# A decoder layer in fp32: one weight split moved behind a bank's copy, and four squares spread out

## The chip, the cores and the metric

The kernel runs on one core of one Trainium2 chip. It is one launch that computes a whole decoder layer. The metric is the device time of that launch in microseconds. The core's engines run side by side, each through its own list of instructions in order: TensorE (PE) multiplies, ScalarE (ACT) and VectorE (DVE) work elementwise, GpSimd (POOL) and SyncE (SP) mostly issue DMAs. An instruction that waits holds up all that stand behind it on its engine.

## The reference

```python
def rms_norm(x, w):
    x32 = x.astype(jnp.float32)
    y = x32 * lax.rsqrt(jnp.mean(x32 * x32, axis=-1, keepdims=True) + EPS)
    return y.astype(x.dtype) * w

def swiglu(h, w_in, w_out):
    gate, up = jnp.split(h @ w_in, 2, axis=-1)
    return (jax.nn.silu(gate) * up) @ w_out
...
        x = x + 0.5 * swiglu(rms_norm(x, norm_ffn1_w[l]), ffn1_w_in[l], ffn1_w_out[l])
        x = x + hybrid_mixer(rms_norm(x, norm_mix_w[l]), ...)
        x = x + memory_cross_attention(rms_norm(x, norm_cross_w[l]), rms_norm(mem, norm_mem_w[l]), ...)
        x = x + 0.5 * swiglu(rms_norm(x, norm_ffn2_w[l]), ffn2_w_in[l], ffn2_w_out[l])
    return rms_norm(x, norm_final_w)
```

x is 512 tokens of 1024 float32 values, the hidden size of both feed-forward networks (FFN1 and FFN2) is 2816, there is one layer, and the memory has 256 tokens. The change touches the two feed-forward networks: their products with `w_in`, and the norm at the start of FFN2.

## The kernel before

**Precision by splitting.** Every float32 operand is split into an upper part in the reduced format fp32r and the lower rest: ScalarE copies the upper part (`wh`, `s31h`, `gh` and so on; the rows of line 155), VectorE subtracts it from the source (`wl`, `s31l`, `gl`; line 156). A product is then three matmuls: upper by upper, upper by lower, lower by upper. A weight tile is 128x1024, and the pools give three buffers each to `wh` and `wl` and six to the raw weights `wr`. So the split of a weight waits until the product three splits earlier has ended.

**A group of seven products.** The FFNs multiply by a scheme of Strassen's kind: `quad` makes a 2x2 block product from seven products instead of eight. Each is 24 matmuls. They run in the order "11" (into bank qa), S1 (qe), S2 (qb), "12" (qa), S3 (qb), S4 (qe), "22" (qb), and each has its own weight split. Between them stand copies of banks: qa is copied to qb after "11" (so that S2 adds to it), qe is saved as `p` after S1, and after S2 qb is saved as `u2` and subtracted from qe (line 300). Only after `u2` is read may S3 write qb. The sums of weights that the products need (`t2`, `t4`) come from VectorE, or, in FFN1, partly from a DMA that accumulates. There are 8 such groups in FFN1 and 11 in FFN2. After a group, `ffn_quads` multiplies by the norm's row, takes the SiLU and multiplies gate and up (lines 447 to 450, tiles `gate` and `th`); `block_tiles` then makes the split sums `g11`, `s31`, `s24` and `g` for the output product.

**The output product.** `out_blocks` does the same seven products for `w_out`, for a third of the hidden size at a time, in parts of two tiles. In FFN1's thirds the weight sums are made on the way: SP loads a part (line 1279), POOL issues an accumulating DMA onto it (line 1318 and, for the last sum, 1336), and VectorE adds the second operand of S2's sum (line 1328), which sets that operand's raw buffer free for a later load.

**The order of the work.** The program is emitted by generators that an `Order` interleaves by an estimated time. A list scheduler then sets the orders of PE, ScalarE and VectorE by its own estimates; SP and POOL keep the order of emission. `behind([...])` forces an instruction behind others of the same engine only. So a weight split under `behind([copy.ins])` has its ScalarE half tied behind that copy, and its VectorE half is free.

**The start of FFN2.** The last part of the cross attention's output (`turn(1)`) writes tiles 4 to 7 of x. The norm of FFN2 needs the squares of all eight tiles (`squared`, line 551), then a row of reciprocal roots (`row_from`, through two small matmuls into `nrow` and the copy of line 407), which the gate multiplies of the first group need. The first group of FFN2 is `fresh`: its first two products are emitted so that their last parts alternate.

Of the kernel before, what the change touches and what calls it, by code (L numbers as in the profile page):

```python
# [13 lines left out]
AF = mybir.ActivationFunctionType  # L14
# [6 lines left out]
KT = D // P  # L21
# [79 lines left out]
def body(tc, a, dbg=None):  # L101
# [13 lines left out]
    def nm(s):  # L115
        uid[0] += 1
        return f"{s}_{uid[0]}"

    def s2(s, dt=F32, shape=(P, T)):
        if math.prod(shape[1:]) <= T // 2:  # L120
            return sp.tile(list(shape), dt, tag="s1", name=nm(s), bufs=NHALF)
        return sp.tile(list(shape), dt, tag="s2", name=nm(s))
# [4 lines left out]
    def small(s, n, bufs=None):  # L127
        return tiny.tile([P, n], F32, tag=s, name=nm(s), bufs=bufs)

    def acc(s, shape=(P, T)):  # L130
        return acc_p.tile(list(shape), F32, tag="acc", name=nm(s))
# [8 lines left out]
    last, start, last_sum, recent, newest, newest_mm = [], [], [], [], [], []  # L140
    V, S, G = nc.vector, nc.scalar, nc.gpsimd
    od = Order()
# [5 lines left out]
    def transpose(out, x):  # L148
        od.t += 2 * (P + 8) / 2400
        nc.tensor.transpose(out, x, ident)  # L150

    def split_into(hi, lo, src, scale=None):
        if scale is None:
            return (
                S.activation(hi, src, AF.Copy),  # L155
                V.tensor_tensor(lo, src, hi.bitcast(F32), ALU.subtract),  # L156
            )
        return (
            S.activation(hi, src, AF.Copy, scale=scale),
            V.scalar_tensor_tensor(lo, src, scale, hi.bitcast(F32), ALU.mult, ALU.subtract),  # L160
        )
# [21 lines left out]
    @contextmanager  # L183
    def behind(ins):
        with ExitStack() as after:
            for i in ins:
                after.enter_context(tc.issue_after(i))
            yield

    H = T // 2  # L190
    S1, S2, S3, S4 = "S1", "S2", "S3", "S4"
# [37 lines left out]
    def add_product(ps, w, xs, which, first, ks=None):  # L229

        wh, wl = w
        n = len(xs)
        for f in range(2):
            out = ps[:, f * H : (f + 1) * H]
            for kp in ks or range(n):
                wc = slice((f * n + kp) * P, (f * n + kp + 1) * P)
                xh, xl = xs[kp][which]
                for j, (a_, b_) in enumerate(((wh, xh), (wh, xl), (wl, xh))):
                    od.t += (H + 32) / 2400
                    newest_mm[:] = [nc.tensor.matmul(out, a_[:, wc], b_, start=first and f == 0 and kp == 0 and j == 0, stop=kp == n - 1 and j == 2, skip_group_check=True).ins]  # L240
                yield

    def raw_w(src, *more):

        raw = wp.tile([P, D], F32, tag="wr", name=nm("wr"), bufs=6)
        nc.sync.dma_start(raw, src)
        for m in more:
            last_sum[:] = [G.dma_start(raw, m, accum_op=ALU.add).ins]
        return raw

    def split_w(raw):
        hi = wp.tile([P, D], R32, tag="wh", name=nm("wh"))
        lo = wp.tile([P, D], R32, tag="wl", name=nm("wl"))
        newest[:] = [split_into(hi, lo, raw)[0].ins]
        return hi, lo

    def quad(xs, src, ready, fresh=False):

        b12, b11, b22, b21 = src[0], src[1], src[2], src[3]
        m1 = raw_w(b11)
        if ready:
            t, t2, m2, m7, m3 = raw_w(ready[0]), raw_w(ready[1]), raw_w(b21), raw_w(b12, b22), raw_w(b22)
            t4 = m2
        else:
            t, m3, m2, m7 = raw_w(b12, b11), raw_w(b22), raw_w(b21), raw_w(b12, b22)  # L270
            t2 = t4 = t
        a_ps = acc("qa")
        e_ps = acc("qe")
        b_ps = acc("qb")
        w1, w5 = split_w(m1), split_w(t)
        second = list(newest)
        if fresh:

            n = len(xs)
            yield from add_product(a_ps, w1, xs, "11", True, range(n - 1))  # L280
            yield from add_product(e_ps, w5, xs, S1, True, range(n - 1))
            yield from add_product(a_ps, w1, xs, "11", False, range(n - 1, n))
            with behind(second):
                S.activation(b_ps, a_ps, AF.Copy)  # L284
            yield from add_product(e_ps, w5, xs, S1, False, range(n - 1, n))
        else:
            yield from add_product(a_ps, w1, xs, "11", True)
            with behind(second):
                S.activation(b_ps, a_ps, AF.Copy)
            yield from add_product(e_ps, w5, xs, S1, True)  # L290
        p5 = s2("p5")
        S.activation(p5, e_ps, AF.Copy)
        if not ready:
            V.tensor_tensor(t2, t, m3, ALU.add)
        yield from add_product(b_ps, split_w(t2), xs, S2, False)
        if not ready:
            V.tensor_tensor(t4, t2, m2, ALU.add)
        u2 = s2("u2")
        S.activation(u2, b_ps, AF.Copy)  # L299
        V.tensor_tensor(e_ps, e_ps, u2, ALU.subtract)  # L300
        yield from add_product(a_ps, split_w(m2), xs, "12", False)
        w7 = split_w(m7)
        if ready:
            V.tensor_tensor(t4, t2, m2, ALU.add)
        yield from add_product(b_ps, w7, xs, S3, False)
        c22 = s2("c22")
        V.tensor_tensor(c22, p5, b_ps, ALU.subtract)
        yield from add_product(e_ps, split_w(m3), xs, S4, False)
        yield from add_product(b_ps, split_w(t4), xs, "22", False)
        yield (a_ps, b_ps), (e_ps, c22)  # L310

# [15 lines left out]
    x, xf, wa = [], [], []  # L327
# [107 lines left out]
    def ffn_quads(xs, wq, st, nq, made, places, sums=None, fresh=False, prime=None):  # L435

        for q in range(nq):
            for out in quad(xs, next(wq), next(sums) if sums else None, fresh and q == 0):
                if out is None:
                    yield  # L440
            gs, us = out
            if prime and q == nq - 1:
                next(prime)
            gate, th = s4("gate"), s4("th")
            for i in range(2):
                row = st.row[:, None, i * H : (i + 1) * H].to_broadcast([P, 2, H])
                V.tensor_tensor(gate[:, 2 * i : 2 * i + 2], halves(gs[i]), row, ALU.mult)
            S.activation(gate, gate, AF.Silu)
            for i in range(2):
                V.tensor_tensor(th[:, places[i]], halves(us[i]), gate[:, 2 * i : 2 * i + 2], ALU.mult)  # L450
            made(th)
            yield
# [97 lines left out]
    def squared(k, src):  # L550
        S.activation(s2("junk"), src, AF.Square, accum_out=squares[:, k : k + 1])

    def row_from(st, apart, rows=1.2):
        both = small("nboth", 4, bufs=2)
        V.tensor_tensor(both, squares[:, :4], squares[:, 4:], ALU.add)
        yield from st.from_sums(both, apart, rows)
# [657 lines left out]
    st_2, xs_2, half = Stat(), [], {}  # L1214
# [20 lines left out]
    def turn(n, banks=None, summed=False):  # L1235

        pt = [bank("pxf") for bank in banks or [aux] * 4]
        for j in range(4):
            for tb in range(4):
                transpose(pt[tb][:, j * P : (j + 1) * P], x[4 * n + j][:, tb * P : (tb + 1) * P])  # L1240
        for tb in range(4):
            S.activation(x[4 * n + tb], pt[tb], AF.Copy)
            if summed:
                squared(4 * n + tb, x[4 * n + tb])
            yield
# [209 lines left out]
            yield from out_blocks(a[f"f2b{c}"], wsum[c], g, col4, ncol4, *((norm, store) if at_end else (None, None)), clean=c == 0)  # L1455

    def turn_last():
        yield from turn(1, summed=True)
        od.spawn(row_from(st_2, 8.0), 3.0)

    od.add(turn_last())
    od.add(ffn2())
    od.run()
# [88 lines left out]
```

## Time and profile before

| | |
|---|---|
| times of the runs | 1314.59, 1314.65, 1318.22 us (median 1314.65) |
| profiled execution | 1314.59 us, of which its span is 1312.7 us |
| TensorE busy | 1288.3 us, 98% of the span |
| VectorE, ScalarE busy | 968.9 us (74%), 708.2 us (54%) |
| granted TensorE clock, mean | 0.997 |
| DMA | 237.38 MB, mean 181 GB/s |

A busy share is an average over the span. Where one engine is busy 98%, what a change can bring is read from the few places where that engine waits, and from which instruction ended each wait. In rows of the profile, `qb<-s31h,wh` means that tile qb is written from tiles s31h and wh; numbers of buffers are left out. `[1.58 <-ACT u L299]` behind a row says that the engine was idle for 1.58 us before it, and that ScalarE's instruction of line 299 that wrote `u` ended this.

### The profile page before, as it was taken

The numbers are of one execution on the slowest core, as the hardware profiler recorded it, in microseconds if no ns is written. First come the engines' busy times: TensorE is split into PE (matmuls) and PEld (weight loads), VectorE is DVE, ScalarE is ACT, GpSimd is POOL, SyncE is SP. The second block draws the span as 40 slices with busy tenths as digits, with TensorE's granted clock in tenths as the row PEclk, the third lists the DMA queues.
The fourth block names the chain that finished last, engine by engine and source line by source line (L and its number), as shares of the span: only waits on it lengthen the run. The fifth ranks groups of instructions, "written<-read, shape, count | busy, mean of one in ns | idle before, by whom it ended". The sixth has DMA issues, their size and how long they took to land.

```text
span 1312.7 us, 20086 instructions
## 1 busy us (share of the span) xinstructions
PE 1288.3 (98%) x7708; PEld 1123.4 (86%) x7708; DVE 968.9 (74%) x1538; ACT 708.2 (54%) x1208; POOL 127.8 (10%) x157
## 2 busy tenths in 40 slices
PE   9999999999999999999999999999999999999996
PEld 7889988998887778777788877888889999989995
DVE  6987887787776676467867686645668878877886
ACT  7544564565754564346645465434375646555564
POOL 0001010001010011201003022020001000000001
PEclk9999999999999999999999999999999999999998
DMA  9366778876984434753466558683239776666762
GB/s 339 88 168 185 212 184 211 222 199 162 324 291 145 137 64 133 261 166 105 95 189 173 167 141 238 196 222 120 69 99 274 209 231 181 185 193 180 201 192 82
DMA packets 70415, 237.38 MB, mean 181 GB/s; under 512 B 8288, under 2 KB 9792, under 8 KB 69968
## 3 DMA queue, kind: packets, MB, share of 16 engines
q1 hardware_dynamic: 54352, 183.20, 41.7%
q0 software_dynamic: 13168, 45.67, 19.7%
q10 hardware_dynamic: 2800, 7.23, 1.7%
q8 instruction: 60, 0.98, 0.3%
q14 instruction: 35, 0.29, 0.1%
HBM read 233.92 MB, written 50.91 MB: 217 GB/s over the span
## 4 chain that ended last, share of the span: by engine, by line
PE 58%; issue 10%; DVE 4%; ACT 2%; DMA 2%; POOL 1%; POOLq 0%; ACTq 0%; DVEq 0%
PE pm L146 10%; PE qb L240 8%; PE qe L240 5%; PE qa L240 5%; PE pxbc L146 4%; PE ob L1298 3%; PE pcq L146 3%; PE pz L146 3%; PE oe L1298 2%; PE oa L1298 2%; PE pcv L146 2%; PE pq L146 2%; PE pv L146 1%; PE pk L146 1%; DMA wr<-in_f1b 1%
## 5 line engine op out<-in xcount | busy, mean ns | idle before, releaser
L155 ACT ACTIVATE wh<-wr 128x1024 fp32r<-128x1024 f32 (+1 forms) x329 | 334.2, 1019 | 359.3 <-issue 70.6
L156 DVE TENSOR_TENSOR wl<-wr,wh 128x1024 fp32r<-128x1024 f32 (+1 forms) x329 | 384.8, 1173 | 145.3 <-ACT wh L155 140.2
L777 ACT ACTIVATE ec<-ec,mn 128x512 f32<-128x512 f32 (+3 forms) x64 | 35.4, 554 | 33.7 <-DVE mn L776 33.7
L146 PE MATMUL pxbc<-hnh,wh 128*128 128x512 f32 x128 | 52.6, 411 | 0.0
L146 PE MATMUL pxbc<-hnh,wl 128*128 128x512 f32 x128 | 50.3, 393 | 0.0
L146 PE MATMUL pxbc<-hnl,wh 128*128 128x512 f32 x128 | 50.2, 392 | 0.0
L240 PE MATMUL qb<-s31h,wh 128*128 128x256 f32 x152 | 43.2, 284 | 3.2 <-ACT u L299 3.2
L240 PE MATMUL qb<-s24h,wh 128*128 128x256 f32 x152 | 43.1, 284 | 1.3 <-ACT qb L284 1.3
L240 PE MATMUL qb<-s24h,wl 128*128 128x256 f32 x152 | 43.1, 284 | 0.5 <-DVE wl L156 0.5
L240 PE MATMUL qe<-s31h,wl 128*128 128x256 f32 x152 | 43.1, 284 | 0.2 <-DVE wl L156 0.2
L240 PE MATMUL qa<-h11h,wh 128*128 128x256 f32 x152 | 43.1, 283 | 0.0
L240 PE MATMUL qa<-h11h,wl 128*128 128x256 f32 x152 | 43.0, 283 | 0.0
L240 PE MATMUL qa<-hmh,wh 128*128 128x256 f32 x152 | 43.0, 283 | 0.0
L240 PE MATMUL qa<-hml,wh 128*128 128x256 f32 x152 | 43.0, 283 | 0.0
L240 PE MATMUL qe<-s24h,wh 128*128 128x256 f32 x152 | 43.0, 283 | 0.0
L240 PE MATMUL qe<-s24l,wh 128*128 128x256 f32 x152 | 43.0, 283 | 0.0
L240 PE MATMUL qe<-s24h,wl 128*128 128x256 f32 x152 | 43.0, 283 | 0.0
L240 PE MATMUL qb<-hmh,wh 128*128 128x256 f32 x152 | 43.0, 283 | 0.0
L240 PE MATMUL qb<-hml,wh 128*128 128x256 f32 x152 | 43.0, 283 | 0.0
L240 PE MATMUL qb<-hmh,wl 128*128 128x256 f32 x152 | 43.0, 283 | 0.0
L240 PE MATMUL qa<-h11l,wh 128*128 128x256 f32 x152 | 43.0, 283 | 0.0
L240 PE MATMUL qa<-hmh,wl 128*128 128x256 f32 x152 | 43.0, 283 | 0.0
(453 smaller groups left out, 4158.3 us busy)
## 6 DMA issues: line engine op xcount, KB each, us to landing
wr<-in_f2q SPq DMA_DIRECT2D x44, 512.0 KB, 4.5
wr<-in_f1q SPq DMA_DIRECT2D x40, 512.0 KB, 4.3
wr<-in_f1b SPq DMA_DIRECT2D x30, 512.0 KB, 4.3
isum<-in_f2q SPq DMA_DIRECT2D x22, 512.0 KB, 6.2
wr<-isum SPq DMA_DIRECT2D x22, 512.0 KB, 4.6
wsum<-in_f2b SPq DMA_DIRECT2D x20, 512.0 KB, 6.7
wr<-wsum SPq DMA_DIRECT2D x20, 512.0 KB, 4.6
wr<-in_f1q POOLq DMA_DIRECT2D x16, 512.0 KB, 6.5
```

The lines of the kernel that those rows point to most:

```text
L146: newest_mm[:] = [nc.tensor.matmul(out, w, x, start=start, stop=stop).ins]
L155: S.activation(hi, src, AF.Copy),
L156: V.tensor_tensor(lo, src, hi.bitcast(F32), ALU.subtract),
L240: newest_mm[:] = [nc.tensor.matmul(out, a_[:, wc], b_, start=first and f == 0 and kp == 0 and j == 0, stop=kp == n - 1 and j == 2, skip_gr ...
L777: S.activation(ec[:, :n], ec[:, :n], AF.Exp, bias=mn, scale=-1.0, accum_out=sm[c][:, i : i + 1])
L1298: newest_mm[:] = [nc.tensor.matmul(ps, a_[:, ts], b_[:, ws], start=first and k == 0 and j == 0, stop=k == n - 1 and j == 2, skip_group_che ...
```

## The change

Two edits. In `quad`, the split of `m3`, the sixth weight of a group (for product S4), is emitted under `behind` of the copy that saves `u2`. In `turn_last`, the squares of tiles 4 to 7 of x are no longer emitted inside `turn(1)`: a chain of its own emits them one by one, each behind the ScalarE half of the newest weight split, 2.0 us of estimated time apart, and then starts the row.

```diff
@@ quad
-        S.activation(u2, b_ps, AF.Copy)
+        copy = S.activation(u2, b_ps, AF.Copy)
         V.tensor_tensor(e_ps, e_ps, u2, ALU.subtract)
...
-        yield from add_product(e_ps, split_w(m3), xs, S4, False)
+        with behind([copy.ins]):
+            w3 = split_w(m3)
+        yield from add_product(e_ps, w3, xs, S4, False)
         yield from add_product(b_ps, split_w(t4), xs, "22", False)
@@ turn_last
-        yield from turn(1, summed=True)
-        od.spawn(row_from(st_2, 8.0), 3.0)
+        yield from turn(1)
+        od.spawn(row_of_last(), 4.0)
+
+    def row_of_last():
+        for k in range(4, KT):
+            with behind(list(newest)):
+                squared(k, x[k])
+            yield 2.0
+        yield from row_from(st_2, 3.0)
```

Line numbers from 308 on are two higher in the changed kernel. What the scheduler makes of it shows in three places.

ScalarE in FFN1, in the third group from the last of its input products. `wh_2800` is the upper half of the sixth split, `wh_2828` of the seventh, `u_494` the copy `u2`; before and after:

```order
L292 ACTIVATE p_487_2683<-qe_2620 128x512
L155 ACTIVATE wh_2800<-wr_2612 128x1024
L155 ACTIVATE s31h_2708<-s_490_2703 128x512
L155 ACTIVATE wh_2828<-wr_2609 128x1024
L299 ACTIVATE u_494_2731<-qb_2621 128x512
L155 ACTIVATE s24h_2747<-s_491_2704 128x512
L155 ACTIVATE gh_2782<-th_2601 128x512
```

```order
L292 ACTIVATE p_487_2683<-qe_2620 128x512
L155 ACTIVATE s31h_2708<-s_490_2703 128x512
L299 ACTIVATE u_494_2731<-qb_2621 128x512
L155 ACTIVATE s24h_2747<-s_491_2704 128x512
L155 ACTIVATE wh_2800<-wr_2612 128x1024
L155 ACTIVATE gh_2782<-th_2601 128x512
L155 ACTIVATE wh_2828<-wr_2609 128x1024
```

The copy has moved ahead of both splits, and the sixth stands behind it and behind `s24h`. In the last group of FFN1 the copy likewise moves ahead of both splits.

ScalarE at the start of FFN2. `junk` rows are the squares, `qb<-qa` the copy after "11", `wh_9940` in the second piece the fourth split; before and after:

```order
L155 ACTIVATE s24h_9799<-s_2042_9790 128x512
L551 ACTIVATE junk_9824,squares_228<-x_119 128x512
L551 ACTIVATE junk_9827,squares_228<-x_121 128x512
L551 ACTIVATE junk_9830,squares_228<-x_123 128x512
L551 ACTIVATE junk_9833,squares_228<-x_125 128x512
L284 ACTIVATE qb_9850<-qa_9848 128x512
L292 ACTIVATE p_2071_9914<-qe_9849 128x512
L155 ACTIVATE wh_9948<-wr_9841 128x1024
```

```order
L155 ACTIVATE s24h_9799<-s_2042_9790 128x512
L553 ACTIVATE junk_9887,squares_228<-x_119 128x512
L155 ACTIVATE wh_9940<-wr_9833 128x1024
L284 ACTIVATE qb_9842<-qa_9840 128x512
L292 ACTIVATE p_2065_9902<-qe_9841 128x512
L553 ACTIVATE junk_9914,squares_228<-x_121 128x512
L553 ACTIVATE junk_9935,squares_228<-x_123 128x512
L155 ACTIVATE wh_9970<-wr_9835 128x1024
```

Three of the four squares have gone behind the copy, and a weight split has come ahead of it.

VectorE in FFN1's last output product. `wr_3458<-wr_3458,wr_3515` is the addition of line 1328 (1330 after) for the second part of S2's sum, `wl_3519` the lower half of the split of that sum; before and after:

```order
L156 TENSOR_TENSOR s31l_3396<-s_596_3390,s31h_3395 128x512
L1328 TENSOR_TENSOR wr_3458<-wr_3458,wr_3515 128x1024
L156 TENSOR_TENSOR s24l_3400<-s_597_3391,s24h_3399 128x512
L1309 SCALAR_TENSOR_TENSOR x_123<-oe_3409,col_67_291,x_123 128x512
L156 TENSOR_TENSOR gl_3404<-th_3380,gh_3403 128x512
L156 TENSOR_TENSOR wl_3495<-wr_3372,wh_3494 128x1024
L160 SCALAR_TENSOR_TENSOR hm_3479<-mem_540_3042,par,hm_3479 128x256
L1309 SCALAR_TENSOR_TENSOR x_125<-oe_3410,col_67_291,x_125 128x512
L160 SCALAR_TENSOR_TENSOR hm_3507<-mem_540_3042,par,hm_3507 128x256
L156 TENSOR_TENSOR wl_3519<-wr_3458,wh_3518 128x1024
```

```order
L1330 TENSOR_TENSOR wr_3372<-wr_3372,wr_3491 128x1024
L156 TENSOR_TENSOR s24l_3400<-s_597_3391,s24h_3399 128x512
L1311 SCALAR_TENSOR_TENSOR x_123<-oe_3409,col_67_291,x_123 128x512
L156 TENSOR_TENSOR gl_3404<-th_3380,gh_3403 128x512
L156 TENSOR_TENSOR wl_3495<-wr_3372,wh_3494 128x1024
L160 SCALAR_TENSOR_TENSOR hm_3479<-mem_540_3042,par,hm_3479 128x256
L1311 SCALAR_TENSOR_TENSOR x_125<-oe_3410,col_67_291,x_125 128x512
L160 SCALAR_TENSOR_TENSOR hm_3507<-mem_540_3042,par,hm_3507 128x256
L1330 TENSOR_TENSOR wr_3458<-wr_3458,wr_3515 128x1024
L156 TENSOR_TENSOR wl_3519<-wr_3458,wh_3518 128x1024
```

The addition has moved down past seven rows and now stands right before the split that reads its result.

## The prediction

> **What bounds the kernel now.** I read the page first, then the waits of TensorE, then the timelines of ScalarE and VectorE around each wait that the change can touch, and last the chain behind the wait in FFN1's last output product. From the page:
>
> ```profile
> span 1312.7 us, 20086 instructions
> PE 1288.3 (98%) x7708; PEld 1123.4 (86%) x7708; DVE 968.9 (74%) x1538; ACT 708.2 (54%) x1208; POOL 127.8 (10%) x157
> PEclk9999999999999999999999999999999999999998
> ```
>
> TensorE is busy 98% of the span at full clock, and the change takes no product away. So it can only earn the few places where PE waits. Those in the three stretches that it reorders:
>
> ```profile
> PE qb L240 <- ACT u L299: 3.2, 2, 1.6
> PE qb L240 <- ACT qb L284: 1.3, 1, 1.3
> PE ob L1298 <- DVE wl L156: 0.5, 1, 0.5
> ```
>
> The first row is two waits of 1.6 us in FFN1's input groups, on the copy u2. The second is the first group of FFN2, on the copy that the four squares stand before. The third is in FFN1's last output product. The first of the u2 waits, ScalarE and then TensorE:
>
> ```profile
> 251.65 1.06 ACT L155 ACTIVATE wh<-wr 128x1024 fp32r<-128x1024 f32 x1 [1.34 <-issue]
> 252.61 0.61 ACT L155 ACTIVATE s31h<-s 128x512 fp32r<-128x512 f32 x1
> 254.54 1.06 ACT L155 ACTIVATE wh<-wr 128x1024 fp32r<-128x1024 f32 x1 [1.31 <-PE qa L240]
> 255.50 0.58 ACT L299 ACTIVATE u<-qb 128x512 f32<-128x512 f32 x1
> ```
>
> ```profile
> 254.28 0.28 PE L240 MATMUL qa<-hmh,wl 128*128 128x256 f32 x1
> 256.13 0.39 PE L240 MATMUL qb<-s31h,wh 128*128 128x256 f32 x1 [1.58 <-ACT u L299]
> 256.36 0.28 PE L240 MATMUL qb<-s31l,wh 128*128 128x256 f32 x1
> 256.47 0.28 PE L240 MATMUL qb<-s31h,wl 128*128 128x256 f32 x1
> ```
>
> The split at 254.54 waits for the end of product "12" (qa), because the weight buffers have three slots; u2, whose bank was complete before "12" began, stands behind it. It should have run during "12". Matmuls follow each other by 0.12 us (0.11 from 256.36 to 256.47, to two places) and a product has 24, so the cover is 2.88 us against a copy of 0.58.
>
> **The change, part by part. First, the sixth split behind u2.** In the new order u2 stands right after s31h in both of these groups, and the seventh split, which waits for "12", comes after it. u2 then ends about 253.8 (s31h's 252.61 + 0.61 + 0.58), before "12" does. Each wait is worth its 1.58 us and the slow first step behind it (256.13 to 256.36 is 0.23 where 0.11 follows), 1.7 us; two make **-3.4 us**. Nothing bigger can come from this edit, since the row of waits has no third.
>
> What the sixth split pays by standing later is seen in an ordinary group of FFN2:
>
> ```profile
> 1024.12 1.06 ACT L155 ACTIVATE wh<-wr 128x1024 fp32r<-128x1024 f32 x1 [0.70 <-PE qb L240]
> 1025.09 0.58 ACT L299 ACTIVATE u<-qb 128x512 f32<-128x512 f32 x1
> 1026.95 1.06 ACT L155 ACTIVATE wh<-wr 128x1024 fp32r<-128x1024 f32 x1 [0.76 <-PE qa L240]
> ```
>
> The first row is the sixth split, the third the seventh. The sixth is used by S4, which begins after S3, some 2.9 us behind the third row. Moved behind u2 and s24h (0.58 and 0.62 us) it still ends near 1026.4, and its lower half (1.22 us) near 1027.7, with 2 us to spare. I take 0 for the other groups; the cover is product S3, and if it went they would cost up to 1 us each, for which no row speaks.
>
> VectorE is less free once PE no longer pauses. In the group after the first wait the new order puts the second gate multiply ahead of a weight split, and in the group with the second wait a gate multiply stands ahead of work for S4:
>
> ```profile
> 295.09 1.22 DVE L156 TENSOR_TENSOR wl<-wr,wh 128x1024 fp32r<-128x1024 f32 x1
> 296.74 0.69 DVE L447 TENSOR_TENSOR gate<-qa,row 128x512 f32<-128x512 f32 x1 [0.43 <-PE qa L240]
> ```
>
> The 295.09 row is the lower half of the sixth split. Now the gate multiply, which waits for "12" until 296.74, comes first; then the subtraction of u2, s24l, and only then this split: 296.74 + 0.60 + 0.60 + 0.60 + 1.22 = 299.8. S4, started 1.7 us earlier than its 301.3 of before, wants it with its third matmul at 299.8. That is between 0 and +0.24. By the same sum of durations the group before it has the lower half for "12" about 0.25 us late (0 to +0.38). I take **+0.4** for both, ends 0 and +0.6.
>
> **Second, the squares in FFN2's first group.**
>
> ```profile
> 976.96 0.61 ACT L551 ACTIVATE junk<-x 128x512 f32<-128x512 f32 x1
> 979.41 0.57 ACT L284 ACTIVATE qb<-qa 128x512 f32<-128x512 f32 x1
> 980.03 0.38 PE L240 MATMUL qb<-s24h,wh 128*128 128x256 f32 x1 [1.33 <-ACT qb L284]
> ```
>
> Four squares run from 976.96 to 979.41, then the copy, then PE. In the new order one square stands before the copy, but so does the fourth weight split, which must wait for product "11" to give back its slot. PE fell idle at 978.70 (980.03 less 1.33) after the last six matmuls of S1, 6 x 0.12, which follow those of "11"; so the slot comes at 977.98, and a split takes 0.96 to the next start (251.65 to 252.61 above). The copy then begins at 978.94 or a little later, I say 978.98, and not at 979.41: **-0.43 us**; ends -1.3 (the wait gone) and 0 (nothing moved). The squares behind the copy also put off the row of the norm:
>
> ```profile
> 987.99 0.60 ACT L407 ACTIVATE row<-nrow 128x512 f32<-128x512 f32 x1 [0.91 <-PE nrow L146]
> 988.96 0.68 DVE L447 TENSOR_TENSOR gate<-qa,row 128x512 f32<-128x512 f32 x1
> 995.18 0.69 DVE L447 TENSOR_TENSOR gate<-qb,row 128x512 f32<-128x512 f32 x1 [0.63 <-PE qb L240]
> ```
>
> The new order has the row's two matmuls 40 matmuls later, 40 x 0.12 = 4.8 us, and both gate multiplies together. Row near 992.9, first gate multiply by 993.6, and the second is held by PE until 995.2 anyway: 0, with 1.6 us of cover. If that went, the SiLU behind it would be late and with it the next group.
>
> **Third, what the diff doesn't show: FFN1's last output product.** The scheduler, given other times, moves one VectorE addition, the second part of the S2 weight sum:
>
> ```profile
> 307.22 0.69 DVE L447 TENSOR_TENSOR gate<-qb,row 128x512 f32<-128x512 f32 x1 [3.51 <-PE qb L240]
> 315.77 1.22 DVE L1328 TENSOR_TENSOR wr<-wr,wr 128x1024 f32<-128x1024 f32 x1
> 320.96 0.48 DVE L160 SCALAR_TENSOR_TENSOR hm<-mem,par,hm 128x256 fp32r<-128x256 f32 x1
> 321.36 1.22 DVE L156 TENSOR_TENSOR wl<-wr,wh 128x1024 fp32r<-128x1024 f32 x1
> ```
>
> Between 307.22 and 321.36 VectorE has no idle row. The addition now stands last, right before the split at 321.36, with the same work ahead, so it ends near 321.4 and not 317.0. Two things hang on it. ScalarE's upper half of that part (1.06 us) ends near 322.5 and the lower half near 323.8:
>
> ```profile
> 322.00 0.39 PE L1298 MATMUL ob<-wh,s24h 128*128 128x512 f32 x1
> 322.90 0.39 PE L1298 MATMUL ob<-wl,s24h 128*128 128x512 f32 x1
> ```
>
> PE wants the upper half at 322.00 and the lower at 322.90: +0.9 to +1.3 here, I take +1.0. And the addition's second operand is a buffer that the next load waits for, at the head of this chain:
>
> ```profile
> 315.86 1.15 DVE wr L1328
> 317.02 4.73 DMA wr<-in_f1b
> 322.37 9.44 DMA wr<-in_f1b
> 331.91 1.07 ACT wh L155
> 333.00 1.24 DVE wl L156
> 334.28 2.58 PE ob L1298 x10
> ```
>
> Addition, SP's load into the freed buffer (4.73 us), POOL's accumulating load onto it, the two halves, PE: this is the wait of 0.5 us of the third row above. Behind that SP load stand two more of its queue, and behind the accumulate two more of POOL's, so all of them shift together. With the addition's end 4.4 us later the SP load is issued at 321.4, lands at 326.2, and the accumulate goes out at 326.8. Its landing is the unknown:
>
> ```profile
> wr<-in_f1q POOLq DMA_DIRECT2D x16, 512.0 KB, 6.5
> wr<-in_f1b POOLq DMA_DIRECT2D x4, 512.0 KB, 11.1
> DMA to landing us min/median/max: 3.6/8.5/16.8
> ```
>
> The first row is the median of the like issues in FFN1's input groups, the second that of the four in this stretch, the third the spread of every load of the stretch, SP's too; 9.44 is the one in question. I take 8.0, between 6.5 and 9.44, because SP's two loads of the stretch will be mostly over by then while the two accumulates behind it still share the engines. Then landing 334.8, halves 2.47 us (331.81 to 334.28 in the chain), PE goes on at 337.3 where it did at 334.28: **+3.0**, which contains the +1.0 (PE arrives late and waits less). With 6.5 it is +1.5, with 9.44 +4.4, with 11.1 +6.1; if the load is no bound at all +0.5, which is the +1.0 less the old 0.5. Behind that every product waits for PE's own results, so I let the shift pass to the end.
>
> [...]
>
> **The sum.** -3.4 + 0.4 - 0.43 + 3.0 = -0.4 us. Made against the profiled execution (span 1312.7, its time 1314.59, 1.9 us lying around the span), which stands 0.06 below the median 1314.65: **1314.2 us**.
>
> **Rivals.** *A, the late load is hidden.* POOL's accumulate lands 5.5 us or less after its issue, and FFN1's last output product pays only 0.5. For it: the stretch's loads begin at 3.6 us. Against it: none of the medians of accumulating loads is that short. Sum -3.4 + 0.4 - 0.43 + 0.5 = -2.9, 1311.7; with VectorE's 0.4 hidden too and the whole FFN2 wait gone, -4.2, 1310.4. [...]
>
> *B, slower: the accumulate crowds.* It goes out when the loads of the next stage (the cross attention's weights) also start, and takes 11.1 us as the median of its neighbours: PE at 340.4, +6.1, sum +2.7, **1317.3**; and its two followers, which landed up to 16.8 us after issue, would then come close to the last product. It turns slower than before when the landing takes longer than 8.4 us (8.0 + 0.4), and passes 0.3% at about 12.4. For it: the median of its own stretch. Against it: that median holds the two followers, which the first does not wait for.
>
> *C, the squares edit doesn't do what it says.* The fourth split takes the squares' place before the copy and waits longer than I think (slot given back late): FFN2 gains 0 and the sum is 0.0, 1314.6.
>
> **How the numbers follow.** My sum with landings between 6.5 and 9.44, C included, has 0.57 and its own range is 1312.7 to 1315.7. A has 0.18, B 0.19, and 0.06 is left for waits at places that I have taken as 0. Eight in ten leave out A's faster half and the worst of B: 1311.0 to 1317.6. A change of 0.3%, 3.9 us, is about what a measurement of this kernel tells from none. Faster than that needs nearly all waits removed and nothing paid: half of A and a little, 0.11. Slower: the worse half of B and most of the unseen waits, 0.15. Within: 0.74.
>
> **What the profile of after would show.** Right: the row of PE waiting for u of the quads is gone; one wait of about 0.9 us stays on the copy at the start of FFN2; PE waits on the weight halves in FFN1's last output product grow from 0.5 to about 3 us, at the second part of S2 and of S3; VectorE's addition there ends about 4.4 us later relative to the gate multiply before it; the SP load and POOL's accumulate follow it by as much. Wrong: u2 waits replaced by waits on wl in S3 or S4 of many groups; no growth in the last output product (A); a landing of over 10 us there (B); a wait for the row before the second group of FFN2.

## The result, and the profile after

The changed kernel is slower: 1319.13 us median over 16 runs (1316.86 to 1322.52) against 1314.97 (1313.51 to 1319.12, 16 runs). The ratio is 1.0029, with a 95% interval of 1.0020 to 1.0037, about 3.8 us. That is outside the predicted range (1311.0 to 1317.6), above its upper end. The profiled execution of after took 1317.88 us with a span of 1315.9, against 1314.59 and 1312.7.

From the page of after, and then its waits of TensorE:

```profile
span 1315.9 us, 20099 instructions
PE 1290.0 (98%) x7708; PEld 1123.7 (85%) x7708; DVE 969.7 (74%) x1538; ACT 707.2 (54%) x1208; POOL 127.6 (10%) x157
```

```profile
PE ob L1300 <- ACT wh L155: 5.3, 2, 4.2
...
PE qb L240 <- ACT qb L284: 0.8, 1, 0.8
...
PE ob L1300 <- DVE wl L156: 0.7, 2, 0.4
...
PE oe L1300 <- DVE s31l L156: 0.5, 2, 0.3
```

The row for `u`, 3.2 us, is gone, and the one on the copy at FFN2's start fell from 1.3 to 0.8. In their place the rows above have 6.5 us of waits in output products (`ob` and `oe`). The kernel before has 1.2 us there: the 0.5 on `wl`, and 0.7 on `s31l` in an earlier third, where the changed kernel still has 0.3. The place of `u2` on ScalarE, in the timeline of the same group as shown of before:

```profile
250.45 0.63 ACT L155 ACTIVATE s31h<-s 128x512 fp32r<-128x512 f32 x1 [1.41 <-DVE s L209]
250.99 0.58 ACT L299 ACTIVATE u<-qb 128x512 f32<-128x512 f32 x1
251.47 0.62 ACT L155 ACTIVATE s24h<-s 128x512 fp32r<-128x512 f32 x1
251.99 1.05 ACT L155 ACTIVATE wh<-wr 128x1024 fp32r<-128x1024 f32 x1
```

The copy ends at 251.57, and product "12" runs until about 253.3: it is hidden, as the change means it to be.

Where the time went can be summed over PE's own starts. Up to the first of the two groups the profiled execution of after is 1.27 us ahead of that of before: 0.53 of it come in the first 105 us, 0.74 in an earlier third's output product (189 to 194 us in the kernel before). Nothing says that this is the change: an execution of a kernel below whose order there is that of before (the late addition alone) is 1.43 us ahead at the same place. Between there and the output product it gains another 3.06. From the first matmul of FFN1's last output product to the end of its last, before takes 40.90 us (307.02 to 347.92) and after 49.29 (302.69 to 351.98): **8.39 us lost in one product**. Another 0.36 are won back behind that product and 0.53 at FFN2's start. -1.27 - 3.06 + 8.39 - 0.36 - 0.53 = +3.17, the difference of the spans (3.2).

In that product, VectorE and ScalarE, then the chain, of after:

```profile
309.27 1.06 ACT L155 ACTIVATE wh<-wr 128x1024 fp32r<-128x1024 f32 x1 [3.34 <-DMA wr<-in_f1b]
...
334.99 1.06 ACT L155 ACTIVATE wh<-wr 128x1024 fp32r<-128x1024 f32 x1 [8.45 <-DMA wr<-in_f1b]
```

```profile
310.37 1.23 DVE L156 TENSOR_TENSOR wl<-wr,wh 128x1024 fp32r<-128x1024 f32 x1 [1.91 <-ACT wh L155]
...
318.03 1.22 DVE L1330 TENSOR_TENSOR wr<-wr,wr 128x1024 f32<-128x1024 f32 x1
320.37 1.22 DVE L156 TENSOR_TENSOR wl<-wr,wh 128x1024 fp32r<-128x1024 f32 x1 [1.12 <-ACT wh L155]
```

```profile
318.11 1.15 DVE wr L1330
319.26 0.02 issue
319.28 6.97 DMA wr<-in_f1b
```

The addition ends at 319.25, its buffer goes to SP's load, that takes 6.97 us, POOL issues the accumulate at 326.87, and ScalarE has the data at 334.99, 8.1 us later. TensorE had come to this place at 331.9:

```profile
331.54 0.39 PE L1300 MATMUL ob<-wl,s31h 128*128 128x512 f32 x1
336.10 0.54 PE L1300 MATMUL ob<-wh,s31h 128*128 128x512 f32 x1 [4.17 <-ACT wh L155]
336.44 0.62 PE L1300 MATMUL ob<-wh,s31l 128*128 128x512 f32 x1
337.36 0.80 PE L1300 MATMUL ob<-wl,s31h 128*128 128x512 f32 x1 [0.30 <-DVE wl L156]
337.96 0.63 PE L1300 MATMUL ob<-wh,s31h 128*128 128x512 f32 x1
338.38 0.63 PE L1300 MATMUL ob<-wh,s31l 128*128 128x512 f32 x1
...
340.21 0.40 PE L1300 MATMUL ob<-wh,s31h 128*128 128x512 f32 x1
```

It waits 4.17 us, and the matmuls behind the wait start 0.43 apart instead of 0.23, until about 339.7. The granted clock (the column after POOL) of that stretch:

```profile
336.00:340.00 4.00, 3.60 (x9) 2.41 (x10) 3.92 (x7) 3.61 (x9) 0.00 (x0) 0.57 1.02 243
```

### The profile page after: what moved, and what is told of

Same layout as the page of the kernel before. It is cut to its first block, busy times and chain, and to the rows that moved or that the text cites. A ratio compares the mean times of both kernels' runs of the same rounds, so it can differ in the third digit from the quotient of the medians.

```text
span 1315.9 us, 20099 instructions
## 1 busy us (share of the span) xinstructions
PE 1290.0 (98%) x7708; PEld 1123.7 (85%) x7708; DVE 969.7 (74%) x1538; ACT 707.2 (54%) x1208; POOL 127.6 (10%) x157
## 4 chain that ended last, share of the span: by engine, by line
PE 74%; issue 13%; DMA 5%; DVE 4%; ACT 2%; POOL 1%; POOLq 0%; ACTq 0%; DVEq 0%
PE qb L240 11%; PE pm L146 10%; PE qa L240 7%; PE qe L240 7%; PE ob L1300 5%; PE pxbc L146 4%; PE pcq L146 3%; PE oa L1300 3%; PE pz L146 3%; DMA wr<-in_f1b 3%; PE oe L1300 3%; PE pa L146 2%; PE pcv L146 2%; PE pg L146 2%; PE pu L146 2%
## 5 line engine op out<-in xcount | busy, mean ns | idle before, releaser
L240 PE MATMUL qb<-s31l,wh 128*128 128x256 f32 x152 | 43.0, 283 | 0.0
L240 PE MATMUL qb<-s31h,wl 128*128 128x256 f32 x152 | 43.0, 283 | 0.0
```

## The experiments

The theory after the result: the whole loss is the late addition in FFN1's last output product and the load chain behind it; the two edits do what they say. The rivals: the squares cost the time; or the stretch is bound by its transfers, so that a TensorE that comes 3 us earlier only waits there instead. All ratios are to the kernel before, measured beside it, with their 95% intervals.

**One edit at a time.** The sixth split behind `u2`, with the squares as before:

```diff
     def turn_last():
-        yield from turn(1)
-        od.spawn(row_of_last(), 4.0)
+        yield from turn(1, summed=True)
+        od.spawn(row_from(st_2, 8.0), 3.0)
...
```

> Only the sixth split behind u2; the squares as before the change. Theory (the loss is made in FFN1's last output product, where one VectorE addition has slid down and its buffer is set free late): like the changed kernel or 0.5 us slower, so 4.0 to 4.5 us over the kernel before (ratio 1.0030 to 1.0034), with the two waits for u2 gone, waits of about 6 us on weight halves in FFN1's last output product, and 1.3 us on the copy at the start of FFN2. Rival (the squares, and the later row of FFN2's norm, cost the time): faster than before by about 3 us (0.9977).

Measured: 1.0045 (1.0031 to 1.0059), more than was expected, though the interval reaches down to it.

```profile
PE ob L1300 <- ACT wh L155: 6.3, 2, 5.2
...
PE qb L240 <- ACT qb L284: 1.3, 1, 1.3
```

And the squares alone, with the split as before (the difference to the changed kernel):

```diff
-        with behind([copy.ins]):
-            w3 = split_w(m3)
-        yield from add_product(e_ps, w3, xs, S4, False)
+        yield from add_product(e_ps, split_w(m3), xs, S4, False)
```

> Only the squares spread out; the sixth split as before. Theory: FFN1 runs as before the change, FFN2's first wait is 0.8 us instead of 1.3, nothing else: 0.4 to 0.5 us faster than before (ratio 0.9996). Rival (the squares cost the time): 3 us or more slower (1.0023 or more).

Measured: 0.9994 (0.9984 to 1.0003).

```profile
PE qb L240 <- ACT u L299: 3.2, 2, 1.6
...
PE qb L240 <- ACT qb L284: 0.8, 1, 0.8
```

The squares are not guilty; their half microsecond is in the trace and too small for this interval. The split alone loses at least as much as both edits together. Its order of instructions in FFN1 is that of the changed kernel, yet its wait was 5.2 us and not 4.2. Counted from the start of the product, TensorE came to the place 0.4 us earlier and the data 0.6 later, of which the accumulate took 8.9 us instead of 8.1. The squares alone have the order of before in FFN1, and yet their execution has 2.0 us of waits in the last output product that before lacks, on weight halves for S4. So one trace of this stretch is certain to a microsecond or two and no better: the order of the instructions does not fix when the loads land.

**The addition put back early.** In the changed kernel, both additions are emitted ahead of the updates of x, and these are tied behind them:

```diff
-            V.tensor_tensor(t_raw[part], t_raw[part], more, ALU.add)
+            add = V.tensor_tensor(t_raw[part], t_raw[part], more, ALU.add)
+            adds.append(add.ins)
...
+        s2_of = sums[2]
+        if by_dma:
+            made = {part: t2(part) for part in parts}
+            s2_of = lambda part: made[part]
-        for t in range(2):
-            update(t + 2, 1, e_ps[t], 1, False)
-        yield from product(b_ps, sums[2], S2)
+        with behind(adds):
+            for t in range(2):
+                update(t + 2, 1, e_ps[t], 1, False)
+        yield from product(b_ps, s2_of, S2)
```

> The changed kernel with the second part's addition of FFN1's last S2 sum forced ahead of the two updates of x, so that it stands two rows behind the first part's. Theory: the addition ends about 4 us earlier than in the changed kernel, SP's load and POOL's accumulate follow it, the wait before the second part of S3 falls from 4.2 us to 1.5 us or less, and the slow matmuls behind it go: 5 us faster than the changed kernel, 0 to 1.5 us faster than before (ratio 0.999 to 1.000). Rival (this stretch is bound by its transfers: PE comes 3 us earlier and the loads don't): the wait stays at 3 us or more, and the time is within 1.5 us of the changed kernel's (1.002 or more).

Measured: 0.9988 (0.9979 to 0.9996), 1314.13 us median. Waits, then the load in the chain:

```profile
PE ob L1300 <- DVE wl L156: 2.7, 2, 2.1
```

```profile
317.03 4.96 DMA wr<-in_f1b
```

The 4.2 us are gone; 0.5 remain before the second part of S3 and a new wait of 2.1 has come in the first part of S2, whose lower half now stands behind both updates. The place of one addition is worth 4.1 parts in a thousand, 5 us, and the transfers are not what costs these 5 us: the rival's 1.002 or more did not come. But the rival is right about something else. TensorE came to this product 3.2 us earlier than in the kernel before and took 3.3 us longer over it, so its lead was gone at the end, and what the two saved waits had brought did not reach the time in this execution.

**A buffer instead of an order.** The addition stays late, but a seventh raw buffer frees the load from it; 12 half-size working tiles instead of 16 make the room. The last two lines stand at three places of the kernel.

```diff
-NHALF = 16
+NHALF = 12
-    tag="wr", name=nm("wr"), bufs=6
+    tag="wr", name=nm("wr"), bufs=7
```

> The changed kernel with seven raw weight buffers instead of six (four half-size working tiles fewer make room); the addition still stands last. SP's load before the second part of S3 then waits for an earlier buffer and not for that addition. Theory: the load goes out 4 us or more earlier, the 4.2 us wait before the second part of S3 is gone or under 1 us, while the wait at the second part of S2 (1.1 us), which comes from the addition itself, stays: about 5 us faster than the changed kernel (ratio to before 0.998 to 1.000). Rival (transfers bound the stretch): the loads go out earlier but land no earlier, and the time is within 1.5 us of the changed kernel's.

Measured: 0.9963 (0.9949 to 0.9977), 1311.0 us.

```profile
PE ob L1300 <- ACT wh L155: 1.0, 1, 1.0
...
PE qb L240 <- ACT qb L284: 0.8, 1, 0.8
```

That is better than expected. In this trace, of the fastest run (1307.82 us), POOL issues the accumulate for the second part of S3 at 314.89, before the late addition has ended (316.02), so that load no longer hangs on it; the first addition comes earlier too (308.96 instead of 312.45). It is not the buffer alone: with the changed pools the scheduler also orders VectorE and ScalarE differently in other places, so the kernel before is needed with the same pools. What stays in the product is the 1.0 us that the late addition costs directly, through the split that reads it.

The same buffers without the change:

> The kernel before with seven raw weight buffers instead of six (four half-size working tiles fewer). It tells what of the 4.9 us that seven buffers gave with the change belongs to the buffers alone. Theory: only the old waits of FFN1's output products go (0.5 and 0.7 us), the two u2 waits and the one at the start of FFN2 stay: 0.5 to 1.5 us faster than before (ratio 0.9989 to 0.9996), so that the change itself is worth 3.4 to 4.4 us on top of it. Rival (more buffers help everywhere, and the change adds nothing to them): 4 us or more faster (0.997 or less).

Measured: 1.0010 (1.0000 to 1.0019), no gain.

```profile
PE pck L146 <- ACT wh L155: 3.4, 1, 3.4
PE qb L240 <- ACT u L299: 3.2, 2, 1.6
...
PE qb L240 <- ACT qb L284: 1.3, 1, 1.3
```

The waits in FFN1's output products went, as expected, but a wait of 3.4 us appeared in the cross attention's first products, which neither the kernel before nor the changed one with seven buffers has. There the split stands on ScalarE behind a copy that waits for a load:

```profile
361.14 0.31 ACT L655 ACTIVATE wdts<-wdt 128x128 fp32r<-128x128 f32 x1 [8.24 <-DMA wdt<-in_wdt]
```

Why that load is late here and not there was not followed. With seven buffers the change is worth 0.9963/1.0010, about 6 us, part of it this wait.

**The late addition alone.** The kernel before, with only the second addition tied behind the second update of x (the scheduler then also moves a few rows of VectorE and ScalarE beside it):

```diff
-            V.scalar_tensor_tensor(x[4 * half_ + tb], src, col, x[4 * half_ + tb], ALU.mult, ALU.add)
+            moved[:] = [V.scalar_tensor_tensor(x[4 * half_ + tb], src, col, x[4 * half_ + tb], ALU.mult, ALU.add).ins]
...
-            V.tensor_tensor(t_raw[part], t_raw[part], more, ALU.add)
+            with behind(moved if by_dma and part == parts[1] else []):
+                V.tensor_tensor(t_raw[part], t_raw[part], more, ALU.add)
```

> The kernel before, with nothing changed but that the second part's addition of FFN1's last S2 sum is tied behind the second update of x, where the changed kernel has it. Theory (the late addition makes the loss by itself): the two waits for u2 stay (3.2 us), the wait before the second part of S3 grows to 4 us or more; with the load and the accumulate as long as in the changed kernel (7.0 and 8.05 us) PE goes on 5 us later than before, and slow matmuls add 1 us: 4 to 7 us slower than before (ratio 1.003 to 1.005). Rival (the loss needs PE to arrive early, so the two saved waits are just moved to this place): under 1.5 us slower (1.001 or less).

Measured: 1.0021 (1.0012 to 1.0029), 2.8 us. Waits, the load, and the clock behind the wait:

```profile
PE ob L1298 <- ACT wh L155: 3.4, 2, 2.4
PE qb L240 <- ACT u L299: 3.2, 2, 1.6
```

```profile
320.50 4.49 DMA wr<-in_f1b
```

```profile
335.00:339.40 4.40, 3.76 (x9) 2.54 (x10) 3.87 (x7) 4.01 (x9) 0.00 (x0) 0.61 1.04 239
```

The late addition makes a loss without any saved wait ahead of it, so the saved waits are not merely moved; but the loss in time is under the 4 us that I had expected as the least. In the trace the product itself took 4.8 us longer than in the kernel before, with a load of 4.49 us and not 7.0. TensorE had come to it 1.45 us earlier, by waits that were absent in FFN1 before it, and so the execution is only 3.0 us longer. How much of the 2.8 us is owed to the shorter load and how much to such a lead, one trace does not tell.

**The slow matmuls.** 16 matmuls that add zero fill the wait in the changed kernel:

```diff
+    zeros_r = cp.tile([P, 16], R32, name="zeros_r")
+    S.activation(zeros_r, ones[:, :16], AF.Copy, scale=0.0)
...
+                if by_dma and which == S3 and part == parts[1]:
+                    for _ in range(16):
+                        nc.tensor.matmul(ps[0], ones_r, zeros_r[:, None, :].to_broadcast([P, 32, 16]), start=False, stop=False, skip_group_check=True)
```

> The changed kernel with 16 matmuls that add zero, 0.227 us each, put before the second part of S3 in FFN1's last output product, to fill most of the 4.2 us in which TensorE waits there; the data comes no earlier. Theory (the six matmuls at about 0.43 us behind that wait, and the mean granted clock of 0.83 in the ten microseconds around it, come from the wait's length): they go, 1.0 to 1.4 us faster than the changed kernel (ratio to before 1.0018 to 1.0025). Rival (they are slow for another reason, a late weight half or a crowded memory port): they stay, and the time is that of the changed kernel within 0.4 us.

Measured: 1.0024 (1.0013 to 1.0035), which can't be told from the changed kernel's 1.0029. In the trace the effect is plain:

```profile
337.10 0.50 PE L1302 MATMUL ob<-wh,s31h 128*128 128x512 f32 x1 [0.98 <-ACT wh L155]
...
340.74 0.39 PE L1302 MATMUL oe<-wh,s24h 128*128 128x512 f32 x1
```

```profile
336.00:341.00 5.00, 3.50 (x15) 2.50 (x15) 3.92 (x7) 4.61 (x9) 0.00 (x0) 1.00 1.05 258
```

From the first matmul behind the wait to the next product it is 3.64 us (337.10 to 340.74), and in the changed kernel 4.80 (336.10 to 340.90): 1.16 us, at a granted clock of 1.00 instead of 0.57. In this execution the data came 1.0 us later (ScalarE at 335.99), which takes the gain away again. The median lies where the theory had put it, but the interval also holds the rival, so the gain is shown by the trace and not by the time.

**Mended versions.** Seven buffers, the early addition, and in FFN2's first group the fourth split tied behind the copy after "11":

```diff
+                first_copy = [S.activation(b_ps, a_ps, AF.Copy).ins]
...
-        yield from add_product(a_ps, split_w(m2), xs, "12", False)
+        with behind(first_copy):
+            w2 = split_w(m2)
+        yield from add_product(a_ps, w2, xs, "12", False)
```

> The changed kernel with three mends: seven raw weight buffers, the second part's addition ahead of the updates of x, and the fourth split of FFN2's first group tied behind the copy after product 11. Theory: the 1.0 us before the second part of S2 and the 0.8 us at the start of FFN2 go: 1.5 to 2 us faster than the changed kernel with seven buffers alone (1311.0), so about 1309.2 (ratio 0.9950). Rival (with the addition early, the first part's lower half is late, as it was with six buffers, 2.1 us): no faster than with seven buffers alone (0.996 or more).

Measured: 0.9946 (0.9933 to 0.9958), 1308.69 us. The wait at FFN2's start is gone. One of 1.1 us is left, in the first part of S2:

```profile
PE ob L1302 <- DVE wl L156: 1.1, 1, 1.1
```

The theory's sum and the rival's wait are both there: the late half came with seven buffers too, though shorter.

Then that half, too, ahead of the updates:

```diff
+            first_w = weights(None, parts[0], made[parts[0]])
+            adds.append(recent[1])
...
-        yield from product(b_ps, s2_of, S2)
+        yield from product(b_ps, s2_of, S2, ready=first_w if by_dma else None)
```

> As the kernel with the three mends (seven buffers, early addition, copy first), and the lower half of the first part's S2 sum is also put ahead of the two updates of x. Theory: the 1.1 us wait in the first part of S2 that those mends left falls under 0.3 us, since two rows of 0.66 us no longer stand before that half: about 0.9 us faster than that kernel (1308.7), so 1307.8 (ratio 0.9939). Rival (the half waits for something else, the raw data or the slot of its buffer): the wait stays, ratio 0.9946.

Measured: 0.9944 (0.9926 to 0.9961), 1307.32 us. No wait of TensorE in the three stretches is left in its list. Between this and the version before it the times don't decide; the trace does, the 1.1 us row is gone.

And the same orders with six buffers:

> The same orders with six raw buffers, so that only the order of instructions is mended: early addition, first half ahead of the updates, copy first in FFN2. Theory: against the kernel with the early addition alone (1314.1, waits of 2.1 us in S2 and 0.8 us at FFN2's start) 1.3 us go from the first and 0.8 from the second: about 1312.2 (ratio 0.997). Rival (the 2.1 us come from a transfer that landed late, at 310.85 us there, and not from the two updates): only the 0.8 us go, 1313.3 (0.998).

Measured: 0.9975 (0.9963 to 0.9987), 1313.12 us, between the two expectations.

```profile
PE ob L1302 <- DVE wl L156: 1.4, 2, 0.8
...
PE ob L1302 <- ACT wh L155: 1.2, 1, 1.2
```

The first part's wait fell from 2.1 to 0.8 us, so by these two traces some two thirds of it were the updates; what remains, and 1.7 us before the second part of S3, comes with six buffers and not with seven. Both mended orders are faster than the kernel before and than the changed one.

## Why the prediction was wrong, step by step

**The two u2 waits, -3.4 us: right.** The row is gone in every kernel with the edit, and stands in the four without it (before, the squares alone, the late addition alone, before with seven buffers). By PE's starts the two are worth 3.67 us, with the slow step behind each.

**VectorE behind them, +0.4: right, at the upper end of its bounds.** PE loses 0.33 us at 270.9 and 0.26 at 297.1, both times on a late weight half, 0.59 together where 0 to 0.6 was allowed; 3.67 less 0.59 is the 3.06 gained, to a few hundredths.

**FFN2's first group, -0.43: right.** The row fell from 1.3 to 0.8 us, 0.53 by starts, and the copy stood behind the fourth split:

```profile
980.71 0.62 ACT L553 ACTIVATE junk<-x 128x512 f32<-128x512 f32 x1
981.23 0.19 ACT L553 ACTIVATION_READ_ACCUMULATOR junk<-x 128x1 f32 x1
981.67 1.06 ACT L155 ACTIVATE wh<-wr 128x1024 fp32r<-128x1024 f32 x1 [0.25 <-PE qa L240]
982.64 0.58 ACT L284 ACTIVATE qb<-qa 128x512 f32<-128x512 f32 x1
```

The later row of the norm cost nothing: the first gate multiply came at 997.20 and the second at 998.41, which PE held up. Tying the split behind the copy took the rest of the wait away.

**FFN1's last output product, +3.0: the mechanism right, the size wrong; it was 8.39.** The accumulate's landing, on which I hung the range and the rivals A and B, came out as I took it: 8.0 us foreseen, 8.1 found. That it came so near is partly luck, since 8.1 is the shortest of the eight kernels with six buffers (8.1 to 9.7). Three other terms of this step failed.

- *"With the same work ahead, so it ends near 321.4."* In the frame of after (4.33 us ahead at this product, 3.06 of it from the change) that is 317.1; it ended at 319.25, 2.2 later. VectorE was idle for 1.91 us before the split at 310.37, whose raw data landed at 309.2. POOL had issued the accumulate for it no earlier than before the change, 300.04 against 299.00, though TensorE was 4.33 us ahead:

```profile
299.00 0.86 POOL L1318 DMA_DIRECT2D wr<-in_f1b  x1 [9.41 <-DVE wl L156]
```

```profile
300.04 0.86 POOL L1320 DMA_DIRECT2D wr<-in_f1b  x1 [9.15 <-DMA wr<-in_f1b]
```

  I had counted VectorE's work as a block that moves with TensorE. Its work moves; the loads that it waits for had not moved. The chain of the changed kernel's trace runs from 280.25 to this addition without a TensorE instruction in it: an accumulate (8.96 us), the two halves of a split, the load that goes out right behind them (291.66, 7.82 us), the accumulate of 300.04 (9.13), the split at 310.37. This also made the unforeseen delays in S1 and the first part of S2, 0.95 and 0.5 us by starts. The rival of the experiments, that the transfers bind, is true for the microseconds by which TensorE was ahead, and does not explain the 5 us that the place of the addition is worth.
- *SP's load, "4.73 us".* It took 6.97. In the changed kernel POOL's accumulate of the part before goes out 1.15 us ahead of it (318.13); in the kernel before it went out 2.4 us behind it (319.44). The runs fall in two sorts: 6.97, 7.08 and 7.27 us with the accumulate 1.0 to 1.2 us ahead (the changed kernel, with zeros, the split alone); 4.73, 4.96 and 4.49 with it 2.4 and 2.8 us behind or 2.9 ahead. Why the load is longer in the first sort these rows do not show; no run moved that accumulate alone.
- *Nothing for TensorE's clock.* The matmuls behind the wait started 0.43 us apart instead of 0.23, which cost 1.16 us.

2.2 + 2.2 + 1.2 is 5.6, and the product cost 5.4 more than foreseen.

**The rivals.** A (the load hidden) did not come with six buffers and did with seven. B was the right side, and near in size (+2.7), by the wrong leg: it let the accumulate take 11.1 us, where the time went into the addition and the load ahead of it. C did not come: the fourth split stands before the copy, as foreseen, and did not wait longer than foreseen. It began at 981.67, which is 977.91 in the frame of before (3.76 us behind there), against a slot foreseen at 977.98.

**The range.** It was built from one unknown, the landing of one transfer, with the two terms ahead of it in the same chain taken as known from the trace before. All three were durations or times of loads under other neighbours, and deserved the same ends: with 6.97 for the load alone the sum would have been +1.8 and not -0.4.

## What to carry to other kernels

A saved wait is worth what stands behind it. Here TensorE came 4.33 us earlier to FFN1's last output product and the work of the other engines followed it, but an accumulate that hung on earlier loads did not (POOL issued it at 300.04, before the change at 299.00), and the list scheduler, given other times, put the one instruction that frees a buffer last. So after each such edit, look for the instruction on which the next load waits, and for whether a buffer more takes that dependence away; here one buffer more, with the orders that came with it, turned 1.0029 into 0.9963, while without the change it gained nothing (1.0010). A load's duration in the trace of before is no more than an estimate for the trace of after: SP's load took 4.73 us in the one, with POOL's accumulate 2.4 us behind it, and 6.97 us in the other, with the accumulate 1.15 us ahead.

## What the runs showed of the hardware that I had not expected

A wait of TensorE cost more here than its length. After 4.17 us idle, matmuls of 512 columns started 0.43 us apart instead of 0.23 for 3 us, at a mean granted clock of 0.57. After the 5.2 us of the kernel with the split alone, 12 started in 6 us, at 0.50, and 15 in the 3 us behind these, at 0.99. After 2.40 us, in the kernel with the late addition alone, as many were slow as after 4.17, at 0.61, and over the next 2.6 us the clock was 1.00. After 2.14 us, in the kernel with the early addition, none were:

```profile
320.00:323.00 3.00, 2.50 (x11) 2.04 (x12) 3.00 (x5) 1.15 (x2) 1.10 (x2) 1.00 0.54 107
```

These are single waits in single executions: whether the length alone decides, and which length, no run here shows. With matmuls that add zero in the wait of the changed kernel, of which 0.98 us was left, the clock was 1.00 from 331 to 341 us.

The accumulate on which the prediction hung its range was the most constant leg of the chain: from POOL's issue to ScalarE's start on its data 8.1 to 9.7 us in the eight kernels with six buffers, before and after among them, where the load ahead of it took 4.5 to 7.3 us in the six in which I read it.
